# Up-projection of a Strassen-Winograd feed-forward: sums of products accumulated in PSUM onto copies placed by ScalarE, with product 1 of the next feature ahead of products 4 and 3

## The chip, the core and the metric

The kernel runs on one core of a Trainium2 chip. Its engines each work through a queue of their own in order and meet through semaphores: TensorE (matmuls, written PE in the profile; PEld are its weight loads), VectorE (DVE), ScalarE (ACT), GpSimd (POOL) and SyncE (SP), which here issues most of the DMA transfers. The metric is the device time of one execution in microseconds (us), lower is better; the time of a kernel is the median of several runs.

## The reference

One layer of a streaming encoder is computed for a prompt of 2048 tokens and for 8 x 16 sample tokens: RMSNorm and one combined projection, chunked attention and an mLSTM side by side, an output projection, and then a convolutional feed-forward network. The change concerns the first matmul of that network:

```python
def conv_ffn(h, buf, w_up, w_conv, b_conv, w_down):      # h: tokens x 1024, w_up: 1024 x 5632
    u = h @ w_up
    ext = concatenate([buf, u], axis=1)
    y = b_conv + sum(ext[:, j:j + S] * w_conv[j] for j in range(3))   # causal depthwise convolution
    gate, up = split(y, 2, axis=-1)
    return (gelu(gate) * up) @ w_down, ext[:, S:]
```

with RMSNorm before and after it and a residual sum. All values are float32.

## The kernel before, in words

Float32 accuracy is reached with three matmuls per product: each operand is split into a high part (float32r) and the remainder, and `mm3` adds high x high, high x low and low x high (lines 95, 96 and 97 of the profile).

*Stages.* The input projection, attention and mLSTM run first, then the output projection (`project`), and beside its end the feed-forward's operands are made. The feed-forward (from line 1263 on) runs over three token blocks, b = 0, 1, 2, of 6, 6 and 5 tiles of 128 tokens. In each block the up-projection loops over 22 features f of 128 columns of the gate and 128 of the up half; its result goes through convolution and GELU and is stored to DRAM (`gd`). Then the down-projection reads it back, in two halves.

*Seven products.* For each f the 1024 x 256 weights and the tokens are cut into 2 x 2 quarters, and four quarters of u come out of seven products (Strassen's scheme in Winograd's form) instead of eight. A product is 4 x 3 = 12 matmuls onto 384 columns (320 in block 2). The token side of the products (`B[P1]` to `B[P3]`) is made once a block; in block 0 the operands of P5, P2, P4 and P3 are kept in DRAM and split late (`late_B`, lines 1151 and 1152). The weight side needs three raw blocks (P1, P2, P4) and four sums of blocks, `ws`. In block 0 VectorE forms the sums (line 1282), and SP stores them (`wsd`) and the later blocks load them from there. The raw float32 blocks and sums sit in 11 `quad` buffers of SBUF and are split into high (ScalarE, line 1265) and low part (VectorE, line 1266) by `load_up`, two groups per feature: P1, P6, P7, P5, then P2, P4, P3. Three sets of buffers hold split groups.

*Sums of products.* With U2 = P1 + P6 the quarters are: gate first half P1 + P2; gate second half U2 + P5 + P3; up first half U2 + P7 + P4; up second half U2 + P7 + P5. Before, ScalarE copies P1 to SBUF (`x1`, line 1489), VectorE adds P6 (`x2`, line 1491) and P7 (`x3`, line 1493). P2 is accumulated in PSUM onto P1, P4 onto P7, P3 onto P5, and VectorE adds x2 or x3 to what stands there (lines 1419 and 1508) on the way to the SBUF tiles `uu` (up) and `ug` (gate); the first half of `ug` is a ScalarE copy (line 1506).

*Convolution.* `conv` copies the halo on GpSimd (lines 1430 and 1435), does one ScalarE activation (line 1438), two VectorE steps (1439 and 1440), and a GELU for the gate (1442). Line 1514 multiplies the two.

*Order.* The programme is written with Tile: it records the operations in the order of the code, and a planner with a timeline of its own decides the order in each engine's queue, so products of neighbouring features are interleaved on TensorE. PSUM has eight banks: two for `a` (tag mm), two for P6's sum (tag sm), two pairs for P7 and P5 (tag big). The down-projection uses mm and big again.

Of the kernel before, what the change touches and what calls it, by code (L numbers as in the profile page):

```python
# [10 lines left out]
F32 = mybir.dt.float32  # L11
# [6 lines left out]
P = 128  # L18
# [26 lines left out]
def hymba_step(ctx: ExitStack, tc: tile.TileContext, I: dict, O: dict):  # L45
# [1224 lines left out]
    def load_quads(b, f, g):  # L1270

        src = lambda i: I["w_up"][f][:, i * 512:(i + 1) * 512]
        if b == 0 and g == 0:
            q = []
            for i in range(4):
                q.append(quad(f"wu{f}_{i}"))
                nc.sync.dma_start(q[i], src(i))
            a11, a12, a22, a21 = q
            s1, s2, s3, s4 = [quad(f"ws{f}_{i}") for i in range(4)]
# [3 lines left out]
            for i, o in enumerate((s2, s3, s1, s4)):  # L1283
                nc.sync.dma_start(wsd[f][:, i * 512:(i + 1) * 512], o)
            raws[f] = [a12, a22, s4]
            return [a11, s2, s3, s1]
        if b == 0:
            return raws.pop(f)
        kept = lambda i: wsd[f][:, i * 512:(i + 1) * 512]
        out = []  # L1290
        for i, s_ in enumerate([[src(0), kept(0), kept(1), kept(2)], [src(1), src(2), kept(3)]][g]):
            r = quad(f"wu{b}_{f}_{g}_{i}")
            nc.sync.dma_start(r, s_)
            out.append(r)
        return out

    def load_up(b, f, g, quads=None):
        n = 2 * f + g
        nm = f"{b}_{f}_{g}"
# [7 lines left out]
        for (h, l), r in zip(at, quads or load_quads(b, f, g)):  # L1307
            split(h, l, r)
        return at
# [75 lines left out]
    pend = [load_up(0, 0, 0)]  # L1385
    late_B()
    pend.append(load_up(0, 0, 1))
# [15 lines left out]
    for b, tiles in enumerate(FBLOCKS):  # L1403
# [13 lines left out]
        def second(u, x, acc):  # L1417

            add = lambda o, c, v=lambda t: t: nc.vector.tensor_tensor(o, v(x[:, c]), v(acc[:, c]), op=ALU.add)  # L1419
            if not last:  # L1420
                add(u[:, 2 + n:2 + 2 * n], slice(0, n))
                return
            add(u[:, 2 + n + 64:2 + n + 192], slice(0, P))
            add(u[:, 2 + n:2 + n + 64], slice(2 * P, n))
            us = u[:, 2 + npr:2 + ln].rearrange("p (b s) -> p b s", b=DB)
            add(us[:, :, 2:DS + 2], slice(P, 2 * P), lambda t: t.rearrange("p (b s) -> p b s", b=DB))
# [18 lines left out]
        def ahead_of(i):  # L1445
            if i < 2 * NF:
                pend.append(load_up(b, i // 2, i % 2))
            elif i == 2 * NF:
                pend.append(load_down(0, 0))
# [27 lines left out]

        for f in range(NF):
            w = pend.pop(0)
            ahead_of(2 * f + 2)  # L1480
# [3 lines left out]
            nm = f"{b}_{f}"  # L1484
            a, d_, ec = ps_mm(f"ua{nm}"), ps_sm(f"ub{nm}"), ps_big(f"uec{nm}")
            e, c = ec[:, 0:512], ec[:, 512:1024]
            x1, x2, x3 = [p4.tile([P, 384], F32, tag="x", name=f"x{i}_{nm}", bufs=3) for i in range(3)]
            product(P1, w[0], a)
            nc.scalar.copy(x1[:, :n], a[:, :n])
            product(P6, w[1], d_)  # L1490
            nc.vector.tensor_tensor(x2[:, :n], x1[:, :n], d_[:, :n], op=ALU.add)
            product(P7, w[2], e)
            nc.vector.tensor_tensor(x3[:, :n], x2[:, :n], e[:, :n], op=ALU.add)
            product(P5, w[3], c)
            uu = u_tile(f"uu{nm}")
            second(uu, x3, c)
            w = pend.pop(0)
            ahead_of(2 * f + 3)
# [5 lines left out]
            ug = u_tile(f"ug{nm}")  # L1504
# [3 lines left out]
            nc.vector.tensor_tensor(uu[:, 2:2 + n], x2[:, :n], e[:, :n], op=ALU.add)  # L1508
# [16 lines left out]
        for dh in range(2):  # L1525
# [9 lines left out]
            for c in range(6):  # L1535
                wh, wl = pend
                if c < 5:
                    pend = load_down(dh, c + 1)
                elif dh == 0:
                    pend = load_down(1, 0)  # L1540
                elif not last:
                    quads = [load_quads(b + 1, 0, i) for i in range(2)]
                    pend = [load_up(b + 1, 0, 0, quads[0])]
# [53 lines left out]
        if not last:  # L1597
            while ahead.step():
                pass
            pend.append(load_up(b + 1, 0, 1, quads[1]))  # L1600
# [94 lines left out]
```

## Time and profile before

| what | value |
|---|---|
| median of 3 runs | 2796.26 us (2793.03 to 2800.73) |
| span of the profiled execution | 2784.7 us; its time beyond the span is not given on the page, and the median of the runs is 11.6 us longer |
| TensorE busy | 2723.8 us, 98% of the span |
| VectorE busy | 1876.3 us, 67% |
| ScalarE busy | 1409.1 us, 51% |
| mean granted clock of TensorE | 0.998 |
| up-projections of blocks 0, 1, 2 | about 1313 to 1641, 1836 to 2154 and 2342 to 2626 us |

The page gives busy time by engine, the granted TensorE clock in slices, DMA queues, the chain of work that ended last, and groups of instructions by source line (`out<-in`, count, busy us, mean ns of one, idle time before them and what ended it). The trace answers further questions: busy time in chosen stretches, who waited for whom, and the instructions in order of time. A busy TensorE counts pipelined matmuls, so its rate is read from the distance of two starts.

### The profile page before, as it was taken

The page shows a single profiled execution, that of the slowest core. Times are in us where ns is not written, and L with a number is a line of the kernel's source. Part 1 is how long each engine was busy: PE and PEld are TensorE (multiplying, and loading weights), DVE is VectorE, ACT ScalarE, POOL GpSimd, SP SyncE. Part 2 cuts the span into 40 slices and gives each one's busy share as a digit, 9 for nine tenths or more (in the row PEclk, how much of TensorE's full clock was granted, in tenths as well). Part 3 has the DMA queues.
Part 4 walks back from the last instruction along what each step waited for, and adds up shares of the span by engine and source line. Part 5 has one row for each costly group of instructions (what it writes and reads, how often), then busy time and mean ns, then how long its engine had stood idle before and what let it go on. Part 6 is the DMA issues. An engine that isn't in the chain of part 4 may idle for free.

```text
span 2784.7 us, 47088 instructions
## 1 busy us (share of the span) xinstructions
PE 2723.8 (98%) x16587; PEld 2548.3 (92%) x16587; DVE 1876.3 (67%) x3447; ACT 1409.1 (51%) x2836; POOL 437.4 (16%) x895
## 2 busy tenths in 40 slices
PE   8999999999999999999999999999999999999998
PEld 7899999998899998888999988899999878999887
DVE  5344455656556668666999986457877864888855
ACT  4355555644356666544454555345455543555543
POOL 1000010212000003244111110011111310222220
PEclk9999999999999999999999999999999999999999
DMA  5544355557555555356655455644544774555585
GB/s 185 155 119 136 103 174 162 164 157 217 162 173 148 144 179 171 107 176 227 187 172 167 167 176 174 219 142 153 160 152 141 276 263 152 172 179 180 192 309 190
DMA packets 311883, 486.05 MB, mean 175 GB/s; under 512 B 55426, under 2 KB 150622, under 8 KB 311518
## 3 DMA queue, kind: packets, MB, share of 16 engines
q1 hardware_dynamic: 271134, 442.92, 50.1%
q10 hardware_dynamic: 38592, 33.83, 3.6%
q0 software_dynamic: 1920, 6.29, 0.6%
q8 instruction: 130, 2.13, 0.3%
q14 instruction: 107, 0.88, 0.1%
HBM read 359.36 MB, written 126.70 MB: 175 GB/s over the span
## 4 chain that ended last, share of the span: by engine, by line
PE 55%; DVE 2%; DMA 1%; issue 1%; ACT 1%; POOL 1%; SPq 0%; DVEq 0%; POOLq 0%; ACTq 0%
PE uec L95 6%; PE uec L96 6%; PE uec L97 6%; PE dn L97 4%; PE dn L96 4%; PE dn L95 4%; PE ua L97 3%; PE ua L95 3%; PE ua L96 3%; PE dnm L97 2%; PE dnm L95 2%; PE dnm L96 2%; PE wo L97 2%; PE wo L95 2%; PE wo L96 2%; PE ub L96 1%
## 5 line engine op out<-in xcount | busy, mean ns | idle before, releaser
L95 PE MATMUL uec<-B,wuh 128*128 128x384 f32 (+1 forms) x720 | 234.9, 328 | 2.2 <-DVE uu L1419 1.1
L96 PE MATMUL uec<-B,wuh 128*128 128x384 f32 (+1 forms) x720 | 235.1, 327 | 0.0
L97 PE MATMUL uec<-B,wul 128*128 128x384 f32 (+1 forms) x720 | 233.9, 327 | 0.0
L1266 DVE TENSOR_TENSOR gl<-gr,gh 128x768 fp32r<-128x768 f32 (+3 forms) x141 | 120.4, 863 | 145.8 <-ACT gh L1265 144.5
L1265 ACT CAST gh<-gr 128x768 fp32r<-128x768 f32 (+3 forms) x141 | 102.0, 735 | 200.1 <-PE dn L96 183.2
L1265 ACT CAST wuh<-wu 128x512 fp32r<-128x512 f32 x255 | 141.7, 617 | 112.1 <-PE uec L96 103.2
L95 PE MATMUL dn<-wdh,gh 128*128 128x512 f32 x466 | 182.4, 391 | 2.3 <-DVE ug L1419 2.3
L96 PE MATMUL dn<-wdl,gh 128*128 128x512 f32 x466 | 183.4, 394 | 0.0
L97 PE MATMUL dn<-wdh,gl 128*128 128x512 f32 x466 | 167.9, 396 | 0.0
L1266 DVE TENSOR_TENSOR wul<-wu,wuh 128x512 fp32r<-128x512 f32 x255 | 164.6, 683 | 2.8 <-DMA x2d<-mx 2.8
L393 DVE CUSTOM_DVE_ANT_0 tmp<-s,nb 128x640 f32<-128x640 f32 (+4 forms) x128 | 94.4, 737 | 96.6 <-PE s L383 94.8
L95 PE MATMUL vo<-wi_h,hT 128*128 128x256 f32 x544 | 155.1, 285 | 0.6 <-DVE mt L199 0.6
L97 PE MATMUL vo<-wi_h,hT 128*128 128x256 f32 x544 | 155.6, 286 | 0.0
L96 PE MATMUL vo<-wi_l,hT 128*128 128x256 f32 x544 | 154.8, 285 | 0.0
L95 PEld LDWEIGHTS uec<-B,wuh 128*128 128x128 f32 x720 | 135.0, 188 | 4.2 <-DVE uu L1419 1.6
L95 PE MATMUL qk<-hT,wi_h 128*128 128x384 f32 (+1 forms) x384 | 128.7, 335 | 7.4 <-ACT qk_st L224 6.6
L96 PEld LDWEIGHTS uec<-B,wuh 128*128 128x128 f32 x720 | 135.2, 188 | 0.2
L97 PEld LDWEIGHTS uec<-B,wul 128*128 128x128 f32 x720 | 135.1, 188 | 0.0
L406 DVE TENSOR_TENSOR ptl<-pt,pth 128x640 fp32r<-128x640 f32 (+4 forms) x128 | 93.6, 737 | 57.1 <-ACT pth L405 56.0
L394 ACT ACTIVATE tmp<-tmp,mn 128x640 f32<-128x640 f32 (+4 forms) x128 | 97.6, 762 | 64.6 <-DVE mn L393 61.9
L96 PE MATMUL qb<-hT,wi_h 128*128 128x384 f32 (+1 forms) x384 | 127.8, 333 | 0.0
L96 PE MATMUL qk<-hT,wi_h 128*128 128x384 f32 (+1 forms) x384 | 127.6, 332 | 0.0
(412 smaller groups left out, 8873.0 us busy)
## 6 DMA issues: line engine op xcount, KB each, us to landing
wu<-in_w_up SPq DMA_DIRECT2D x220, 256.0 KB, 4.1
wu<-wsd SPq DMA_DIRECT2D x176, 256.0 KB, 4.2
wdr<-in_w_down SPq DMA_DIRECT2D x132, 256.0 KB, 5.6
gr<-gd SPq DMA_DIRECT2D x78, 384.0 KB, 3.6
wi_raw<-in_w_in SPq DMA_DIRECT2D x52, 512.0 KB, 4.0
wsd<-ws SPq DMA_DIRECT2D x88, 256.0 KB, 2.8
gd<-g SPq DMA_DIRECT2D x44, 384.0 KB, 3.5
kraw<-kTd SPq DMA_DIRECT2D x112, 128.0 KB, 3.2
```

The lines of the kernel that those rows point to most:

```text
L95: nc.tensor.matmul(out, ah, bh, start=start, stop=False, skip_group_check=onto)
L96: nc.tensor.matmul(out, ah, bl, start=False, stop=False, skip_group_check=onto)
L97: nc.tensor.matmul(out, al, bh, start=False, stop=stop, skip_group_check=onto)
L393: nc.vector.tensor_tensor_reduce(o_, s_, b_, 1.0, 3e38, ALU.add, ALU.min, accum_out=mn)
L394: nc.scalar.activation(tmp[:, :n], tmp[:, :n], AF.Exp, bias=mn, scale=-1.0, accum_out=rsum[:, i % 4, hh:hh + 1])
L406: nc.vector.tensor_tensor(s.ptl[:, sl, qc], ptv, s.pth[:, sl, qc], op=ALU.subtract)
L1265: nc.scalar.copy(h, r)
L1266: nc.vector.tensor_tensor(l, r, h, op=ALU.subtract)
```

## The change

1. The sums U2, U2 + P5 and so on are no longer added by VectorE. The copy of P1 goes from PSUM to PSUM, into the first bank of a `big` pair (`dc`), and P6 is accumulated onto it. ScalarE copies that sum (U2) into the second bank, and P5 is accumulated onto it. P4 is accumulated onto the first bank, P3 onto the second. P7 has a bank of its own (tag sm) and ScalarE copies it to SBUF (`p7`).
2. VectorE keeps two adds per feature: p7 + second bank (after P5) and p7 + first bank (after P4). The second half of `ug` is a ScalarE copy after P3.
3. Product 1 of feature f + 1 and its copy are written before P4 and P3 of feature f. So the weight groups are cut anew: P6, P7, P2, P5 of a feature, then P1 of the next with P4 and P3. In block 0 the block of P1 is loaded with its group, before the other raw blocks of its feature.
4. Before block 0 four matmuls write the four banks of the `big` tiles once with start=True (`mark`), so that later matmuls without it add to what stands there.
5. `quad` has 12 buffers instead of 11, `row` 6 instead of 4; the room comes from `dynamic_dma_scratch_size=4096`, a smaller area for the descriptors of GpSimd's DMAs.

```diff
 def quad(name):
-    return ffn.p3.tile([P, 512], F32, tag="q", name=name, bufs=11)
+    return ffn.p3.tile([P, 512], F32, tag="q", name=name, bufs=12)
 def row(name):
-    return ffn.p3.tile([P, D], F32, tag="yq", name=name, bufs=4)
+    return ffn.p3.tile([P, D], F32, tag="yq", name=name, bufs=6)
...
+    GROUPS_UP = [[(P1, 0), (P6, 0), (P7, 0), (P2, 0)], [(P5, 0), (P1, 1), (P4, 0), (P3, 0)]]
+    for f_ in range(1, NF):
+        GROUPS_UP.append([(P6, f_), (P7, f_), (P2, f_), (P5, f_)])
+        GROUPS_UP.append([(P1, f_ + 1)] * (f_ + 1 < NF) + [(P4, f_), (P3, f_)])
...
+    def first_quads(i, f):
...
+        if i == P1:
+            get(P1, 0)
+        elif i == P6:
+            a12, a22, a21 = get(P2, 1), get(P4, 2), get(None, 3)
+            a11 = raws["a11"] if f else raws[P1, 0]
+            s1, s2, s3, s4 = [quad(f"ws{f}_{x}") for x in range(4)]
...
-        def second(u, x, acc):
-            add = lambda o, c, v=lambda t: t: nc.vector.tensor_tensor(o, v(x[:, c]), v(acc[:, c]), op=ALU.add)
+        def halves(u, x, acc):
...
+        def first(f):
+            a, dc = ps_mm(f"ua{b}_{f}"), ps_big(f"udc{b}_{f}")
+            product(P1, W.pop((P1, f)), a)
+            nc.scalar.copy(dc[:, :n], a[:, :n])
+            return a, dc[:, 0:512], dc[:, 512:1024]
+
+        if b == 0:
+            for i in range(2):
+                t = ps_big(f"mark{i}")
+                for x in range(2):
+                    nc.tensor.matmul(t[:, x * 512:x * 512 + 384], B[P1][:, 0, 0, :P], B[P1][:, 0, 0, :],
+                                     start=True, stop=True)
...
-            product(P1, w[0], a)
-            nc.scalar.copy(x1[:, :n], a[:, :n])
-            product(P6, w[1], d_)
-            nc.vector.tensor_tensor(x2[:, :n], x1[:, :n], d_[:, :n], op=ALU.add)
-            product(P7, w[2], e)
-            nc.vector.tensor_tensor(x3[:, :n], x2[:, :n], e[:, :n], op=ALU.add)
-            product(P5, w[3], c)
-            second(uu, x3, c)
+            product(P6, W.pop((P6, f)), d_, onto=True)
+            nc.scalar.copy(c[:, :n], d_[:, :n])
+            product(P7, W.pop((P7, f)), e)
+            nc.scalar.copy(p7[:, :n], e[:, :n])
+            product(P2, W.pop((P2, f)), a, onto=True)
+            nc.scalar.copy(ug[:, 2:2 + n], a[:, :n])
+            product(P5, W.pop((P5, f)), c, onto=True)
+            for o, x, y in halves(uu, p7, c):
+                nc.vector.tensor_tensor(o, x, y, op=ALU.add)
...
-            product(P2, w[0], a, onto=True)
-            nc.scalar.copy(ug[:, 2:2 + n], a[:, :n])
-            product(P4, w[1], e, onto=True)
-            nc.vector.tensor_tensor(uu[:, 2:2 + n], x2[:, :n], e[:, :n], op=ALU.add)
-            product(P3, w[2], c, onto=True)
-            second(ug, x2, c)
+                nxt = first(f + 1)
+            product(P4, W.pop((P4, f)), d_, onto=True)
+            nc.vector.tensor_tensor(uu[:, 2:2 + n], p7[:, :n], d_[:, :n], op=ALU.add)
             yu = conv(uu, 1, f)
+            product(P3, W.pop((P3, f)), c, onto=True)
+            for o, _, y in halves(ug, None, c):
+                nc.scalar.copy(o, y)
             yg = conv(ug, 0, f)
...
-    nc = bacc.Bacc("TRN2", target_bir_lowering=False, num_devices=1)
+    nc = bacc.Bacc("TRN2", target_bir_lowering=False, num_devices=1, dynamic_dma_scratch_size=4096)
```

More of the change, by code (lines that the diff above doesn't have):

```diff
@@ L1541, in hymba_step @@
                 elif not last:
-                    quads = [load_quads(b + 1, 0, i) for i in range(2)]
-                    pend = [load_up(b + 1, 0, 0, quads[0])]
+                    quads = [load_quads(b + 1, i) for i in range(2)]
+                    pend = [load_up(b + 1, 0, quads[0])]
                 ks = list(range(4 * c, 4 * c + (4 if c < 5 else 2)))
```

97 lines of the change are left out of this document (53 added, 44 removed).

## The prediction

> **What bounds the kernel now.** I read the page first, then busy time by stage for the feed-forward part (it starts at 1313 us), then TensorE's waits there.
>
> ```profile
> span 2784.7 us, 47088 instructions
> ...
> PE 2723.8 (98%) x16587; PEld 2548.3 (92%) x16587; DVE 1876.3 (67%) x3447; ACT 1409.1 (51%) x2836; POOL 437.4 (16%) x895
> ```
>
> ```profile
> core 0: us, PE busy (x) PEld busy (x) DVE busy (x) ACT busy (x) POOL busy (x), PEclk, DMA share, GB/s
> 1313.00:1641.00 328.00, 322.00 (x1827) 318.55 (x1825) 302.79 (x457) 167.79 (x266) 61.74 (x87) 0.99 0.54 179
> 1641.00:1836.00 195.00, 193.23 (x865) 157.51 (x864) 110.03 (x152) 94.51 (x158) 6.71 (x22) 1.00 0.55 181
> 1836.00:2154.00 318.00, 318.00 (x1826) 317.91 (x1825) 246.19 (x366) 163.19 (x270) 42.99 (x96) 1.00 0.48 154
> 2154.00:2342.00 188.00, 186.85 (x837) 151.25 (x836) 120.16 (x156) 88.56 (x150) 36.99 (x46) 1.00 0.68 231
> 2342.00:2626.00 284.00, 283.56 (x1904) 280.91 (x1902) 244.50 (x493) 160.17 (x284) 64.43 (x182) 1.00 0.56 177
> 2626.00:2785.00 159.00, 148.00 (x636) 119.34 (x636) 89.40 (x129) 60.06 (x107) 30.61 (x41) 0.99 0.72 253
> ```
>
> Rows one, three and five are the up-projections of blocks 0, 1 and 2, the part that the change rewrites. TensorE is busy for 318.00 of 318 us in block 1 and 283.56 of 284 in block 2: nothing can be won there unless matmuls go away, and none does. Block 0 alone has a hole, 6 us, and there VectorE is busy for 302.79 of 328 us (92%), because it also forms the weight sums. Stage edges apart, the whole possible gain lies in block 0. Its waits:
>
> ```profile
> engine line waited for: us in total, times, longest us
> PE ua L97 <- DVE wul L1266: 3.0, 2, 1.6
> PE uec L95 <- DVE uu L1419: 1.1, 1, 1.1
> PE uec L95 <- DVE ug L1419: 1.0, 1, 1.0
> PE ub L97 <- DVE wu L1266: 0.6, 1, 0.6
> ...
> PE uec L95 <- DVE x L1493: 0.3, 1, 0.3
> PE uec L95 <- DVE uu L1508: 0.2, 1, 0.2
> ```
>
> These six rows are the up-projection's: 6.2 us, each wait ended by VectorE. The matmul pitch and the worst stall, from the timeline of TensorE, and that stall's clock, by windows:
>
> ```profile
> 1639.67 0.34 PE L96 MATMUL uec<-B,wuh 128*128 128x384 f32 x1
> ...
> 1640.88 0.34 PE L97 MATMUL uec<-B,wul 128*128 128x384 f32 x1
> ```
>
> ```profile
> 1387.08 0.42 PE L95 MATMUL uec<-B,wuh 128*128 128x384 f32 x1 [0.96 <-DVE ug L1419]
> ...
> 1389.06 0.69 PE L97 MATMUL ua<-B,wul 128*128 128x384 f32 x1 [1.39 <-DVE wul L1266]
> ```
>
> ```profile
> 1389.00:1392.20 3.20, 3.14 (x10) 3.14 (x11) 3.20 (x7) 0.38 (x1) 0.51 (x1) 0.54 0.68 210
> ```
>
> Seven starts apart is 1.21 us, so 0.173 us a matmul, 2.08 us a product of 12, 14.5 us a feature. After 0.96 and 1.39 us of waiting the granted clock was 0.54 for 3.2 us, which lost 3.2 x 0.46 = 1.5 us more. So block 0 loses 6.2 + 1.5 = 7.7 us. [...]
>
> What the worst stall and the next one followed, in the chain of waits:
>
> ```profile
> 1378.67 6.98 DMA wu<-in_w_up
> ...
> 1386.85 0.95 DVE g L1514
> ...
> 1388.41 0.61 DVE wul L1266
> 1389.06 0.69 PE ua L97
> ```
>
> ```profile
> 1514.25 5.42 DMA wu<-in_w_up
> ```
>
> A weight load took 6.98 us to land, VectorE stood before the weight sum that needs it, and then had its queue to work off.
>
> **The change, part by part.** Costs of what moves, block 0's rows by shape, VectorE then ScalarE:
>
> ```profile
> L1491 DVE TENSOR_TENSOR x<-x,ub 128x384 f32<-128x384 f32 x22 | 12.0, 547 | 0.1
> L1493 DVE TENSOR_TENSOR x<-x,uec 128x384 f32<-128x384 f32 x22 | 12.0, 545 | 0.0
> L1419 DVE TENSOR_TENSOR ug<-x,uec 128x384 f32<-128x384 f32 x21 | 11.5, 549 | 4.4 <-PE uec L97 4.3
> L1152 DVE TENSOR_TENSOR B<-B 128x1536 fp32r<-128x1536 f32 x4 | 6.8, 1745 | 0.0
> ```
>
> ```profile
> L1442 ACT ACTIVATE y<-y 128x768 f32<-128x768 f32 x20 | 16.9, 847 | 53.1 <-DVE y L1440 53.1
> ...
> L1489 ACT COPY x<-ua 128x384 f32<-128x384 f32 x22 | 10.5, 479 | 16.0 <-PE ua L97 16.0
> ```
>
> *Adds removed, copies added.* Per feature VectorE loses three adds, 1.64 us, 36 us over block 0's 22 features: 303 - 36 = 267 of 328 us, 81%. ScalarE gains three copies. A copy from PSUM to PSUM is not in the trace; the nearest row is L1489's of the same width, PSUM to SBUF, 0.479 us, and I take that (bounds: half of it, and the 0.847 us of a row twice as wide, L1442's): 22 x 3 x 0.48 = 32 us, 168 + 32 = 200 us, 61%, at the upper bound 68%. In block 2 the upper half of ug takes three small copies in place of three small adds. Neither engine becomes the bound by its sum. Worth on the path: only the VectorE waits after block 0's start, 0.96 + 1.39 + 1.1 + 0.3 + 0.2 = 3.9 us, and the clock's 1.5: 5.4 us. They began with late loads, so they are not sure to go; but a VectorE with 19% to spare works off its queue, and the rearranged groups (the twelfth quad buffer, product 1's block loaded one group ahead) let the third raw block be fetched about one group, 7 us, sooner. I take 4.3 of the 5.4; the ends are 0 and 5.4.
>
> *New waits: P1 -> copy -> P6, and P6 -> copy -> P5.* Two round trips in each of 66 features. TensorE's queue behind the waiting matmul is in order, so all later products wait with it. A trip costs the pipeline's tail (0.34 - 0.17), the start of the copy and the copy. The start is seen here:
>
> ```profile
> 1843.69 0.34 PE L97 MATMUL ua<-B,wul 128*128 128x384 f32 x1
> ...
> 1844.07 0.48 ACT L1489 COPY x<-ua 128x384 f32<-128x384 f32 x1 [1.18 <-PE ua L97]
> ```
>
> 0.04 us after the end, so with as much at the other end 0.17 + 0.04 + 0.48 + 0.04 = 0.73 us. In the built order 23 or more other matmuls stand between, mostly 24 (two products, 4.15 us) to 36, past the first features of each block. Cover left: 3.4 us. What can eat it is ScalarE's own order: a copy behind a GELU that waits for VectorE's convolution. Those waits (ScalarE, up-projections 0, 1, 2 in turn):
>
> ```profile
> ACT y L1442 <- DVE y L1440: 53.1, 17, 5.1
> ```
>
> ```profile
> ACT y L1442 <- DVE y L1440: 14.5, 13, 1.7
> ```
>
> ```profile
> ACT y L1442 <- DVE y L1440: 21.2, 13, 3.0
> ```
>
> Means 3.1, 1.1 and 1.6 us, longest 5.1, 1.7 and 3.0: only block 0 can pass 3.4. With less on VectorE the waits should shorten, and in the built order the GELU belongs to an older feature, whose convolution has mostly run. I take +0.7; the ends are 0 and 22 x (5.1 + 0.73 - 4.15) = 37 us.
>
> *Starts of blocks 1 and 2.* There only one product (2.08 us) stands between the first P1 and P6, so 1.35 us of cover, and ScalarE is still squaring the down-projection's rows, here before:
>
> ```profile
> 1841.40 0.64 ACT L1344 ACTIVATE junk<-fr 128x512 f32<-128x512 f32 x1
> ```
>
> One square ahead of the copy fits, three do not. I take +0.3 a block, +0.6; the ends are 0 and the whole product twice, 4.2.
>
> *Start of block 0.* Four mark matmuls, 4 x 0.173 = +0.7 us on TensorE. The four late operands are split on VectorE (L1152, 1.745 us each). The first was needed after five products, now after four, 2.1 us sooner; in the new order ScalarE and VectorE have less else in between. Before, the waits at this place were 1.6 + 0.6 = 2.2 us. Ends: -2.2 if they vanish, +2.1 if all of the lost cover shows. I take +0.6, nearer to the upper end than the middle is, because VectorE is the engine waited for.
>
> *The rest, at nothing.* SP issues the same transfers; product 1's block moves ahead of four sums and their stores. POOL copies halos as before, the gate's now first; it is busy for 62 of 328 us. Smaller descriptor scratch concerns POOL's 24 output stores in the down stages, where POOL is busy for 7 of 195 and 37 of 188 us; if one waited there, 150 us of idle cover it. More row buffers can only start loads earlier. At the end of each block the last down-projection sums wait for the evacuation of P3, now a ScalarE copy: 0.48 for 0.55 us, +/-1 us over three edges.
>
> **Sum:** -4.3 + 0.7 + 0.6 + 0.7 + 0.6 = -1.7 us on a span of 2784.7, so 2783.0. The page gives no more of that execution than its span; the median of the runs, 2796.26, is 11.6 us above it, and I keep that distance: 2794.6 us.
>
> **Rivals.**
> 1. *ScalarE's order stalls TensorE (slower).* Copies stand behind GELUs, and it decides as soon as GELU waits pass 3.4 us. For: 17 waits of 3.1 us on average in block 0. Against: VectorE gets 19% spare. If half of the 17 last 5.1 us, 8.5 x 1.7 = 14 us, in place of 0.7: 2794.6 + 13.3 = 2808 us. Chance 0.17.
> 2. *All waits go, edges included (faster).* Block 0's 7.7 and the later edges:
>
> ```profile
> PE dnm L95 <- ACT gh L1265: 1.8, 2, 1.5
> PE dn L95 <- DVE ug L1419: 1.6, 2, 1.4
> ```
>
> 3.4 us more, by the added quad and row buffers; with 0.7 for the marks -10.4: 2786 us. Against: the edges' work is unchanged. Chance 0.13.
> 3. *The stalls are the loads' and stay.* Both chains hold a late load that the lighter VectorE does not hasten. Without the 4.3: 2799 us. Chance 0.20.
> The forecast itself has 0.50.
>
> **How the numbers follow.** Within 0.3% (8.4 us, about what a measurement of this kernel can tell from no change; its three runs spread over 7.7 us) lie the forecast and rival 3: 0.70. Slower by more: rival 1, 0.17. Faster by more: rival 2, 0.13. The range runs from rival 2's 2786 less 1 us to 2805, most of the way to rival 1; the copies' upper end of 37 us is left outside.
>
> **What would show it.** Right: VectorE at some 267 us and ScalarE at 200 in block 0's up-projection, TensorE's waits there under 4 us, no row of a matmul of udc waiting for ScalarE by more than a us in total, and no window at half clock. Wrong: many waits of udc matmuls for the copies at L1504 or L1525, with GELU waits above 3 us ahead of them; a wait over 3 us at block 0's first P2 or P5; or blocks 1 and 2 no longer without a wait.

## The result, and the profile after

The changed kernel takes 2799.29 us (median of 20 runs, 2793.89 to 2807.54) against 2794.68 us for the kernel before, measured beside it (20 runs, 2792.06 to 2800.90): a ratio of 1.0015, 95% interval 1.0009 to 1.0022. It is slower by 4.6 us, where 1.7 us less was forecast. The time lies inside the forecast range, and the difference is smaller than the 0.3% that was called measurable; twenty runs of each resolve it all the same, and its sign is the wrong one.

Its profiled execution has a span of 2794.9 us. The spans of single executions mislead:

```profile
core 0: 2784.7 us, clock 0.998
```

```profile
core 0: 2796.1 us, clock 0.994
```

Both rows, from the view of spans and mean granted clock, are of the kernel *before*: the first is the execution that the prediction read, the second another one. The lost clock, 0.002 of 2785 us against 0.006 of 2796 us, makes 11 us, which is the difference of the spans. In the first execution TensorE reached its first up-projection matmul at 1313.45 us, in the second at 1323.72, with the same instructions up to there. So up to that matmul a single profile is worth 10 us of chance, and kernels are compared from that matmul on. The stages of five kernels, three of which come below (each figure is the distance between two starts in the timeline of TensorE: the first up-projection matmul of a block, the first of the down-projection after the block's last one, or the end):

| us | block 0 up | down | block 1 up | down | block 2 up | down | sum |
|---|---|---|---|---|---|---|---|
| before (mean of two traces) | 338.8 | 184.0 | 329.2 | 183.7 | 278.2 | 158.0 | 1471.9 |
| changed (mean of two traces) | 340.3 | 184.3 | 331.5 | 183.6 | 280.0 | 157.7 | 1477.3 |
| copies alone (e7) | 334.3 | 184.2 | 331.1 | 183.3 | 280.2 | 159.0 | 1472.1 |
| and VectorE at the block ends (e8) | 335.8 | 183.8 | 330.8 | 183.0 | 279.0 | 158.4 | 1470.7 |
| and the add moved (e15) | 331.9 | 183.8 | 330.3 | 184.6 | 279.0 | 156.7 | 1466.2 |

The changed kernel loses 5.4 us there, and 0.7 us for the marks ahead of it: 6.1 us by the traces, 4.6 us by the medians. Busy time by stage, in the changed kernel's first trace (the cut points are its own stage starts):

```profile
core 0: us, PE busy (x) PEld busy (x) DVE busy (x) ACT busy (x) POOL busy (x), PEclk, DMA share, GB/s
1318.00:1648.00 330.00, 324.06 (x1837) 321.45 (x1837) 275.91 (x395) 195.01 (x336) 61.41 (x88) 0.99 0.54 179
...
1842.00:2164.00 322.00, 321.15 (x1839) 320.11 (x1838) 220.40 (x306) 190.56 (x339) 44.02 (x97) 1.00 0.50 154
...
2357.00:2628.00 271.00, 270.22 (x1840) 269.38 (x1839) 206.98 (x369) 179.17 (x381) 68.21 (x182) 1.00 0.57 176
```

The work moved about as forecast: VectorE from 303 to 276 us in block 0 (267 was forecast), ScalarE from 168 to 195 (200). TensorE still stands for 6 of 330 us in block 0, but elsewhere than before. Its waits there, and then at the ends of blocks 0, 1 and 2:

```profile
PE ua L96 <- DVE B L1152: 2.8, 1, 2.8
PE ue L97 <- DVE wu L1266: 1.1, 1, 1.1
PE ua L95 <- ACT B L1151: 1.1, 1, 1.1
PE udc L95 <- DVE uu L1534: 0.7, 1, 0.7
```

```profile
PE dn L95 <- ACT ug L1549: 1.9, 1, 1.9
```

```profile
PE h2T_pt L1093 <- DVE x2r L1085: 1.2, 1, 1.2
PE udc L95 <- DVE uu L1534: 0.7, 1, 0.7
```

```profile
PE dn L95 <- ACT ug L1549: 2.0, 1, 2.0
PE udc L95 <- DVE uu L1534: 0.8, 1, 0.8
```

None of the 3.9 us of waits that block 0 had after its start is left. The first three rows are all of the start: 5.0 us, against 2.2 before. The clock behind them, by windows:

```profile
1331.40:1338.30 6.90, 4.85 (x14) 4.34 (x15) 6.26 (x5) 3.50 (x6) 1.90 (x2) 0.51 0.54 211
```

For 6.9 us TensorE had 0.51 of its clock; it was busy for 4.85 us of them, so some 2.4 us were lost (4.85 x 0.49). Windows of 3.4 us at half clock also stand behind the ends of blocks 0 and 2 in both of its traces; of before's two, one has such a window, behind block 2. In the changed kernel's first trace they start at 1659.05 and 2638.67 us. Place by place for block 0: -3.9 of waits and -1.5 of clock, then +2.8 at the start, +2.4 of clock behind it, and at the end +1.3 for the first down-projection sum (1.95 against 0.65) and about as much as before around it. That is +1.1; the two pairs of stage lengths say +1.5. The 0.65 us are in TensorE's timeline of the kernel before:

```profile
1652.39 0.50 PE L95 MATMUL dn<-wdh,gh 128*128 128x512 f32 x1 [0.65 <-DVE ug L1419]
```

Blocks 1 and 2 lose 2.2 and 1.8 us, most of it at their ends (0.7 us in block 1 lie at 2104 us, in four gaps that the trace gives no wait for).

What the worst wait hangs on, in the chain of waits, which gives start, us and what:

```profile
1324.75 1.42 ACT B L1151
1326.17 2.08 ACT wuh L1265 x4
1328.25 0.37 ACT p L1527
1328.62 1.38 ACT B L1151
1330.02 3.24 DVE B L1152
1333.31 0.69 PE ua L96
```

The late operands are copied by ScalarE and split by VectorE in the order product 5, 2, 4, 3. That order was left from the kernel before, where product 5 came first. The changed kernel needs product 2's first. So product 2 stands on ScalarE behind the copy of an operand that is not yet wanted and behind four weight casts (that operand's split on VectorE is over 0.6 us before product 2's begins). And its own split takes 3.24 us, where the prediction priced it at 1.745 us. The reason shows when VectorE's and GpSimd's timelines are laid side by side:

```profile
1327.66 1.75 DVE L1152 TENSOR_TENSOR B<-B 128x1536 fp32r<-128x1536 f32 x1
1330.02 6.57 DVE L1152 TENSOR_TENSOR B<-B 128x1536 fp32r<-128x1536 f32 x3 [0.61 <-ACT B L1151]
```

```profile
1327.83 3.81 POOL L1027 TENSOR_TENSOR mx<-mx 128x1024 f32<-128x1024 f32 x1 [1.40 <-DVE mx L1026]
```

GpSimd's residual add of the last row starts 0.17 us after the first split and takes 3.81 us, where the same add for the two rows before it took 2.4 us; it ends at 1331.64. The second split starts inside it and ends 1.6 us after it, at 1333.25. The other two take 1.75 us again. When the add started, 1.58 us of the first split were left, and the add took 1.41 us more than 2.4; when the second split started, 1.62 us of the add were left, and the split took 1.48 us more than 1.75. So the lengths come out as if each of the two instructions had stood still for nearly all that was left of the other.

### The profile page after: what moved, and what is told of

Its sections match the earlier page's. It is cut to its first block, busy times and chain, and to the rows that moved or that the text cites. A ratio compares the mean times of both kernels' runs of the same rounds, so it can differ in the third digit from the quotient of the medians.

```text
span 2794.9 us, 46904 instructions
## 1 busy us (share of the span) xinstructions
PE 2732.2 (98%) x16591; PEld 2556.6 (91%) x16591; DVE 1790.6 (64%) x3205; ACT 1482.9 (53%) x3078; POOL 441.2 (16%) x895
## 4 chain that ended last, share of the span: by engine, by line
PE 56%; DVE 1%; DMA 1%; ACT 1%; issue 1%; POOL 1%; SPq 0%; DVEq 0%; POOLq 0%; ACTq 0%
PE udc L95 6%; PE udc L96 6%; PE udc L97 6%; PE dn L97 4%; PE dn L96 4%; PE dn L95 4%; PE ua L96 3%; PE ua L97 3%; PE ua L95 3%; PE dnm L97 2%; PE dnm L95 2%; PE dnm L96 2%; PE ue L97 2%; PE ue L96 2%; PE ue L95 2%; PE wo L97 2%
## 5 line engine op out<-in xcount | busy, mean ns | idle before, releaser
L95 PE MATMUL udc<-B,wuh 128*128 128x384 f32 (+1 forms) x720 | 235.7, 328 | 2.2 <-DVE uu L1534 2.2
L96 PE MATMUL udc<-B,wuh 128*128 128x384 f32 (+1 forms) x720 | 235.6, 327 | 0.0
L97 PE MATMUL udc<-B,wul 128*128 128x384 f32 (+1 forms) x720 | 235.3, 327 | 0.1
L96 PE MATMUL dn<-wdl,gh 128*128 128x512 f32 x466 | 184.6, 396 | 0.0
L95 PEld LDWEIGHTS udc<-B,wuh 128*128 128x128 f32 x720 | 135.5, 188 | 3.4 <-DVE uu L1534 3.3
L97 PEld LDWEIGHTS udc<-B,wul 128*128 128x128 f32 x720 | 135.4, 188 | 0.7 <-DVE wul L1266 0.7
L96 PEld LDWEIGHTS udc<-B,wuh 128*128 128x128 f32 x720 | 135.5, 188 | 0.1
L97 PE MATMUL qk<-hT,wi_l 128*128 128x384 f32 (+1 forms) x384 | 128.2, 334 | 0.0
```

Source lines behind the costliest of these rows:

```text
L95: nc.tensor.matmul(out, ah, bh, start=start, stop=False, skip_group_check=onto)
L96: nc.tensor.matmul(out, ah, bl, start=False, stop=False, skip_group_check=onto)
L97: nc.tensor.matmul(out, al, bh, start=False, stop=stop, skip_group_check=onto)
```

## The experiments

All ratios are against the kernel before, run on the same chip. The theory at the outset (A): the loss is three places, the start of block 0, the ends of the blocks, and the half clock behind both. Its rivals: ScalarE's copies cost it all along (B), or chance does. Further ones came up on the way and are named in the expectations.

**e0: the changed kernel again.**

> The changed kernel once more, beside the kernel before and the next three on one chip. Every theory expects the ratio of its first measurement, 1.0015 (1.0009 to 1.0022), some 4 us above the kernel before. What the profile should repeat, if the theory holds that the edit itself makes three kinds of loss (A): some 5 us of TensorE waits for VectorE at the start of block 0's up-projection, two waits of about 2 us for the ScalarE copy of ug at the ends of two blocks, and windows of 3.4 us at half clock behind both. By the rival (B) that these are chance of one execution, they should be shorter or absent in a second profile.

2797.33 us, ratio 1.0025 (1.0017 to 1.0034). The second trace repeats the first: waits of 1.13, 1.08 and 2.82 us at the start with 6.8 us of half clock behind them, 1.95 and 2.05 us at the ends of blocks 0 and 2, each stage within 0.8 us. The losses belong to the kernel and not to one execution.

**e1: six products ahead of the late operands.**

```diff
-    GROUPS_UP = [[(P1, 0), (P6, 0), (P7, 0), (P2, 0)], [(P5, 0), (P1, 1), (P4, 0), (P3, 0)]]
+    GROUPS_UP = [[(P1, 0), (P6, 0), (P7, 0), (P1, 1)], [(P2, 0), (P5, 0), (P4, 0), (P3, 0)]]
...
+            if f == 0:
+                take(1)
             product(P2, W.pop((P2, f)), a, onto=True)
```

> The changed kernel with the first two weight groups of block 0 regrouped, so that six products instead of four stand before the first product that needs a late operand; nothing else is changed. Theory A (the start lost its cover): the TensorE waits at the start of block 0, 5.0 us in the changed kernel's trace, fall to 2 us or less, the two half-clock windows behind them (3.4 us lost) go, and the median falls by 4 to 7 us, to a ratio of 0.999 to 1.000 against the kernel before. Rival B (the loss comes from ScalarE's added copies and the round trips all along the three blocks): the ratio stays at 1.0015.

2799.45 us, ratio 1.0032 (1.0020 to 1.0045): no gain over e0. The start did improve, and the half-clock windows there went, but block 0 took 339.8 us:

```profile
PE udc L95 <- DVE uu L1545: 2.3, 2, 1.9
PE dn L95 <- ACT ug L1549: 1.9, 1, 1.9
PE ue L97 <- DVE wul L1266: 1.5, 2, 0.8
PE udc L95 <- DVE uu L1534: 1.0, 2, 0.7
PE ua L96 <- DVE B L1152: 1.0, 1, 1.0
PE ua L95 <- ACT B L1151: 0.8, 1, 0.8
```

The last two rows are the start, 1.8 us in place of 5.0. What VectorE did not owe at the start it owes one feature later, for uu (1.9 us at 1349) and for weight splits at 1439 and 1616. "The start lost its cover" was right about the wait and wrong about the time.

**e2, e3: VectorE copies ug at the ends of the blocks; e3 with the start of e1.**

```diff
-                nc.scalar.copy(o, y)
+                (nc.vector.tensor_copy if f == NF - 1 else nc.scalar.copy)(o, y)
```

> The changed kernel, but the last feature of each block has the second half of ug copied by VectorE instead of ScalarE. Theory A: at the ends of the blocks ScalarE stands at three or four casts of down-projection weights of 1.66 us each when P3's sums are ready, VectorE does not; the two waits of 1.95 and 2.04 us shrink to 0.7 to 1.4 us each, the half-clock windows behind them become fewer, and the median falls by 1 to 5 us. Rival B: the waits at these places end with the weights, so that a wait of the same 2 us for ScalarE's casts takes their place and the time stays.

> Both edits together: regrouped start and VectorE's copy at the ends of the blocks. Theory A: the gains add up, 5 to 12 us below the changed kernel, so 1 to 8 us below the kernel before: a ratio of 0.997 to 0.9997, since what is left of the edit is the 4.3 us that VectorE's waits in block 0 cost, less 0.7 us for the marks. Rival B: no better than the changed kernel, 1.0015.

Ratios 1.0014 (1.0005 to 1.0022) and 1.0012 (1.0003 to 1.0020), where e0 has 1.0025 on that chip: 1.3 and 1.0 us less by the medians, but the intervals overlap. From the first up-projection matmul on, e2's trace is 1475.0 us long, against 1476.7 and 1477.9 in the changed kernel's two. In e2's trace the wait at the end of block 0 is

```profile
PE dnm L95 <- ACT gh L1265: 0.8, 1, 0.8
PE dn L95 <- DVE ug L1549: 0.7, 1, 0.7
```

and no half-clock window follows it. What the copy had waited for in the changed kernel is in ScalarE's timeline:

```profile
1655.99 1.66 ACT L1265 CAST wdh<-wdr 128x512 fp32r<-128x512 f32 x3 [4.12 <-PE udc L96]
1657.55 0.47 ACT L1549 COPY ug<-udc 128x384 f32<-128x384 f32 x1
```

Three weight casts, 1.66 us, stood ahead of a copy of 0.47 us in ScalarE's queue. By the traces the exchange takes back 1.8 to 2.9 of the 5.4 us lost; the medians alone don't settle it. e3 (forecast 0.997 to 0.9997) missed, as e1 did.

**e4, e7, e8: accumulation onto copies, the rest undone.** e4 restores the old weight groups and puts product 1 back at the head of its own feature; e7 also restores the three sizes; e8 adds the exchange of e2 to e7.

```diff
-            if f == 0:
-                nxt = first(0)
+            nxt = first(f)
...
-            else:
-                nxt = first(f + 1)
```

> The changed kernel with the weight groups of the kernel before and without running product 1 ahead: product 1 stands again at the head of its own feature, products 4 and 3 come before it; the accumulation onto ScalarE's copies stays. Only one product then stands between product 1 and product 6 in program order, though the built order has 23 to 25 other matmuls between most of them. If the round trips cost nothing wherever a product or two stand between (theory A), the steady parts of the blocks show no wait for the copies, the start of block 0 waits 2 us instead of 5, and the ratio falls to 0.999 to 1.001. If running ahead is what hides the trips (rival E), TensorE waits at product 6 or product 5 for ScalarE in many features, tens of us in all, and the ratio is above 1.003.

> The accumulation onto ScalarE's copies alone, with everything else of the edit undone: old weight groups, product 1 at the head of its own feature, 11 quad buffers, 4 row buffers, the default descriptor scratch. Theory C' (the sizes cost some 4 us in block 0 through another order of the same work, and the copies themselves gain): block 0's up-projection with its edge takes 335 to 338 us against 338.8 of the kernel before, and the ratio is 0.998 to 1.000. Rival F (the copies cost it, whatever the sizes: ScalarE's evacuation at the three block ends and the wait for uu's sum there): blocks 1 and 2 keep their 2 us each, block 0 gains nothing, and the ratio is 1.0015 or more.

> The same, with VectorE in place of ScalarE for the copy of the second half of ug in the last feature of each block. Theory C': about 1.5 us below the kernel with ScalarE's copy, as the same exchange gave on the changed kernel; a ratio of 0.997 to 1.000 against the kernel before, the waits of the first down-projection sums 0.65 to 0.8 us instead of 2. Rival F: 1.001 or more.

Ratios 1.0006 (0.9997 to 1.0015), 1.0014 (1.0004 to 1.0023) and 0.9997 (0.9987 to 1.0008). In none of them does TensorE wait for the copies of L1504 or L1525 (the numbers in these kernels differ by a few lines); running product 1 ahead is not what hides the trips, since the built order puts 22 or more other matmuls between most of them in either case. So rival E is out, and since e8 has all the copies and shows no loss, so is rival B. Theory A gave e4 a start with 2 us of waits; its trace has 4.4 us there (0.2, 1.7, 0.5 and 1.9), and block 0 takes 340.3 us. e7's waits from its first up-projection matmul to the end of block 0's edge:

```profile
PE ue L97 <- DVE wu L1266: 2.7, 1, 2.7
PE dn L95 <- ACT ug L1543: 1.9, 1, 1.9
PE udc L95 <- DVE uu L1529: 0.5, 1, 0.5
PE ua L95 <- ACT B L1151: 0.3, 1, 0.3
```

Nothing is left between the start and the end: in this trace block 0 is 4.5 us shorter than before, and blocks 1 and 2 are each 2 us longer. In e8, whose TensorE order is the same up to the end of block 0, the gain there is 3.0 us: a half-clock window follows its wait of 2.7 us, and none follows e7's. e8 takes back 0.3 and 1.2 us in blocks 1 and 2 and can't be told from the kernel before. Rival F is right about the ends, and wrong that block 0 gains nothing. By the medians e7 is 3.5 us behind the kernel before, as F forecast and theory C' did not; its one trace shows 0.9 us (0.2 in the stages, 0.7 for the marks).

**e5, e6, e9, e10: the sizes.** e6 is the kernel before with all three new sizes, e9 with the quads alone, e10 with the rows alone (both with the smaller scratch, which was not run alone; e10 has it and loses nothing); e5 is the changed kernel with the old ones.

```diff
-        return ffn.p3.tile([P, 512], F32, tag="q", name=name, bufs=11)
+        return ffn.p3.tile([P, 512], F32, tag="q", name=name, bufs=12)
```

> The kernel before with nothing changed but the three sizes: 12 quad buffers, 6 row buffers, descriptor scratch of 4096. In the five traces of the changed kernel and its variants TensorE reaches the up-projection 3.6 to 7.7 us later than in the one trace of the kernel before, though the instructions up to there are the same; most of it comes between 440 and 1040 us. Theory C (the sizes delay the earlier stages): this kernel also reaches the up-projection some 4 us late, and its ratio to the kernel before is 1.001 to 1.002. Theory D (the one trace of before was an undisturbed execution, the lateness there is chance that any execution has): ratio 1.0000, give or take 0.0008, though its single profile may be late as well.

> The changed kernel with the three sizes of the kernel before: 11 quad buffers, 4 row buffers, the default descriptor scratch. Theory C (the sizes delay the earlier stages): the median falls by some 4 us against the changed kernel, to a ratio of 1.000 to 1.001 against the kernel before, unless loads in block 0 become later in exchange. Theory D (the sizes do nothing there): the ratio stays at 1.0015 to 1.0025, or rises where the twelfth quad buffer was needed: then the profile shows more TensorE waits for weight sums in block 0.

> The kernel before with 12 quad buffers instead of 11 (and the smaller descriptor scratch that makes the room), 4 row buffers as before. With both sizes the ratio was 1.0015 and block 0's up-projection took 3.7 us longer. If the twelfth quad buffer is the cause, it is 1.001 to 1.002 again, with a wait of some 3 us for a weight sum's low part at the start of block 0 as there; if the row buffers are, it is 1.0000, give or take 0.0008.

> The kernel before with 6 row buffers instead of 4 (and the smaller descriptor scratch), 11 quad buffers as before. The counterpart of the kernel with the quad buffer alone: 1.001 to 1.002 if the row buffers are the cause, 1.0000 if the quad buffer is. In both, the earlier stages are free to be 0 to 10 us late in a single profile, which then says nothing about the sizes.

e6 1.0015 (1.0005 to 1.0025), e9 1.0029 (1.0019 to 1.0038), e10 0.9996 (0.9987 to 1.0005), e5 1.0049 (1.0030 to 1.0068). The twelfth quad buffer alone costs the kernel before as much as the whole edit, and not in the earlier stages, as Theory C had it; Theory D's 1.0000 for e6 is out too. By the traces block 0 takes 3.7 us more in e6 and 1.9 us more in e9; the rest of e9's 5.5 us lies in the down-projection of block 1 (2.1 us) and in block 2 (1.4 us), and its cause stays open. The two longest of e9's waits in block 0:

```profile
PE ua L97 <- DVE wul L1266: 3.7, 2, 3.0
PE uec L95 <- DVE x L1493: 2.1, 2, 1.4
```

The buffer changes no instruction. It changes the order in which the planner sets them. At the place where TensorE waited 1.6 us for a weight split before, it now waits 3.0 us: that split stands behind the late operands' splits, one of which takes 3.50 us here beside GpSimd's add of 3.85 us, and starts 19.4 us after the first up-projection matmul instead of 17.4 (in before's second trace). Taken away from the changed kernel together with the other two sizes, it costs far more (e5: block 0's up-projection 350.6 us, 10 us of half clock at its start). Between e4 and e7, which differ in the sizes alone, the medians show no gain, though e7's trace is 4 us shorter. So the buffer is neither good nor bad: each order meets the start of block 0 in its own way.

**b0: the kernel before again.**

> The kernel before once more, for a second profile. Theory D: the profile is 2788 to 2793 us long, with some of the lateness between 440 and 1040 us and more than two half-clock windows ahead of the tail. Theory C: it again reaches the up-projection at about 1313.5 us.

Ratio 1.0006 (0.9997 to 1.0016): no difference, as it must be, and a measure of what such a comparison tells apart. On the lateness its trace settles Theory D against C: 1323.72 us to the first up-projection matmul, 10.3 us later than in the first trace, and 6 half-clock windows up to there instead of 1, which is 8.5 us of it. (With 2796.1 us its span is even longer than D's 2788 to 2793.)

**e12, e13: product 2's operand first; e13 with VectorE at the ends.**

```diff
-        for i in (P5, P2, P4, P3):
+        for i in (P2, P5, P4, P3):
```

> The changed kernel with the late operands loaded and split in the order in which its products now need them: product 2's first, product 5's second (the code kept 5, 2, 4, 3 from the time when product 5 came first). Theory I (the loss at the start of block 0 is this order): the waits at the start fall from 5.0 us to some 2 us, with one half-clock window fewer or two, block 0's up-projection falls from 340 to 335 to 337 us, and the ratio from 1.0015-1.0025 to 1.0000-1.0010. Rival J (the twelfth quad buffer's order of work costs it, whatever operand comes first): the ratio stays at 1.0015 or above.

> Product 2's operand first, and VectorE's copy of the second half of ug at the ends of the blocks. Theory I with the gain of the exchange seen twice (about 1.3 and 3.9 us): a ratio of 0.998 to 1.000 against the kernel before, with block 0's up-projection at 334 to 336 us. Rival J: 1.0012, as with the regrouped start.

1.0012 (1.0003 to 1.0022) and 1.0006 (0.9997 to 1.0016). The wait for product 2's operand fell from 3.9 us in two pieces to 0.3, and no half-clock window is left at the start. But the built order changed with it, so that e12's block 0 still took 340.4 us, with new waits of 0.5 and 0.2 us for the round-trip copies, 0.7 us for product 5's split (3.27 us long beside the add) and 2.0 us for weight splits. Theory I holds for the wait, and rival J for the time of block 0; the ratio lies between their forecasts.

**e11: one instruction moved, all else equal.**

```diff
-            nc.gpsimd.tensor_tensor(xr, m, xr, op=ALU.add)
+            (nc.gpsimd if nxt else nc.vector).tensor_tensor(xr, m, xr, op=ALU.add)
```

> The changed kernel with one instruction moved: the last row's add of 128x1024 into the residual goes from GpSimd to VectorE; every other order on every engine stays. In the changed kernel that add runs from 1327.83 for 3.81 us, and the split of product 2's operand on VectorE takes 3.23 us beside it instead of 1.75. Theory G (the two engines block each other there, and TensorE's wait of 2.83 us at product 2 contains that 1.5 us): the split takes 1.75 us, TensorE's wait at product 2 falls by about 1 us although VectorE has 1.3 us more to do, and the kernel is 1 to 3 us faster if a half-clock window goes with it. Rival H (the long split is a matter of its data's place, or of the load): it takes 3.2 us again and the wait grows by 1.3 us.

2793.14 us, ratio 1.0010 (1.0001 to 1.0019). VectorE's timeline:

```profile
1327.66 1.75 DVE L1152 TENSOR_TENSOR B<-B 128x1536 fp32r<-128x1536 f32 x1
1329.33 1.22 DVE L1027 TENSOR_TENSOR mx<-mx 128x1024 f32<-128x1024 f32 x1
1330.46 5.09 DVE L1152 TENSOR_TENSOR B<-B 128x1536 fp32r<-128x1536 f32 x3
```

Three splits take 5.09 us in place of 6.57. TensorE's waits in block 0:

```profile
PE ua L96 <- DVE B L1152: 1.8, 1, 1.8
PE udc L97 <- DVE wul L1266: 1.4, 1, 1.4
PE ue L97 <- DVE wu L1266: 1.1, 1, 1.1
PE ua L95 <- ACT B L1151: 1.1, 1, 1.1
PE udc L95 <- DVE uu L1534: 0.7, 1, 0.7
PE ua L97 <- DVE wul L1266: 0.4, 1, 0.4
```

The wait at product 2 is 1.8 us in place of 2.8: Theory G to a tenth of a us. The next one, for a weight split, took up more than was won: the start waits 5.8 us in all, against 5.0. But the longest single wait is a us shorter, and no half-clock window stands at the start any more, nor behind block 0's end, where the 1.95 us wait is unchanged. By the traces the kernel is 4 to 5 us shorter from the first up-projection matmul on (1472.7 against 1476.7 and 1477.9). The ratio's interval overlaps with those of the changed kernel, so the medians alone do not settle the gain; the split's duration does settle the collision.

**e14, e15, e16: the repaired versions.** e14 is e8 with six row buffers; e15 is e8 with e11's move; e16 is e13 with it.

> The accumulation onto copies with the old groups, 11 quad buffers and VectorE's copy at the ends (0.9997 so far), with 6 row buffers, which alone came out at 0.9996. If the two are independent: 0.9985 to 1.000. If the six row buffers only looked harmless with the adds in place: above 1.000.

> The accumulation onto copies with old groups and old sizes and VectorE's copy at the block ends (0.9997 so far), with the last row's 128x1024 add on VectorE instead of GpSimd. There the add ran beside two weight splits, which took 3.49 us instead of 1.28, and TensorE waited 2.69 us for a later one. Theory G: the two splits take 1.3 us, the wait falls by some 0.9 us (2.2 saved less 1.3 for the add), and the ratio is 0.998 to 0.9995. Rival: what is gained there is given back at the next wait, and it stays at 0.9997.

> Product 2's operand first, VectorE's copy at the block ends (1.0006 so far), and the last row's add on VectorE. The split beside the add took 3.28 us instead of 1.75, and three waits near it lasted 0.3, 0.5 and 0.7 us. Theory G: at most 1 us less, a ratio of 0.9995 to 1.0005; by the rival that block 0's later waits and the 0.9 us at each block end are the rest of the loss, it stays above 1.000 and blocks 1 and 2 keep their 1.4 and 0.5 us.

e14 1.0001 (0.9991 to 1.0011), e16 0.9999 (0.9988 to 1.0009): neither can be told from the kernel before. e16 is the changed kernel with all three repairs. Within these intervals they take back its whole loss, which fits the start and the ends as its cause; the move of the add may also gain something of its own, as in e15. e15 beats both kernels: 2785.80 us against 2792.00, ratio 0.9974 (0.9964 to 0.9983). In e8 two weight splits beside the add took 3.49 us; in e15 the same two take 1.28. First e8's row, then e15's:

```profile
1324.34 3.49 DVE L1266 TENSOR_TENSOR wu<-ws,wu 128x512 fp32r<-128x512 f32 x2
```

```profile
1323.34 1.28 DVE L1266 TENSOR_TENSOR wu<-ws,wu 128x512 fp32r<-128x512 f32 x2
1324.55 1.22 DVE L1027 TENSOR_TENSOR mx<-mx 128x1024 f32<-128x1024 f32 x1
```

and its waits in block 0 and at its end are

```profile
PE udc L95 <- DVE uu L1529: 1.1, 2, 0.6
PE dn L95 <- DVE ug L1543: 0.7, 1, 0.7
PE ua L95 <- ACT B L1151: 0.5, 1, 0.5
PE udc L95 <- DVE uu L1539: 0.3, 1, 0.3
```

The 2.7 us wait of e7 and e8 is gone whole, not by the 0.9 us worked out ahead, and a few TensorE rows changed places as well, which may be why; block 0 is 6.9 us shorter than in the kernel before. The add was not moved in the kernel before alone, though the same collision stands there: beside the add one of its 128x512 splits takes 2.44 us, where it takes 0.68 alone. So the rival that the move by itself gives all of e15's gain is not tested, and how much of the gain needs the copies stays open: e8, which has them without the move, shows no gain over the kernel before.

## Why the prediction was wrong

*VectorE's waits in block 0, -4.3 (ends 0 and -5.4).* Right, and at its better end. All of 3.9 us and the half-clock window behind them are gone in both traces of the changed kernel; e7, where the copies and the marks are all that is new, has a block 0 shorter by 4.5 us, its slower end included (e8's and e14's, with the same 2.7 us wait and a half-clock window behind it, by 3.0). But the lighter VectorE alone doesn't ensure it: in e1, with the same copies in another order, 4.2 us of such waits stand past the start. Rival 3, that these waits belong to the loads, is out: the loads of weights took longer to land after the change (5.1 us in the median against 4.1 over the whole kernel, 5.1 against 4.9 in block 0's up-projection), and the waits went all the same.

*Round trips, +0.7.* The copies from PSUM to PSUM took 0.47 us, where 0.48 was taken. The waits were zero in the changed kernel, where no row names L1504 or L1525 as what TensorE waited for; 0.7 to 3.2 us in e12 and e5, whose orders put less between. The cover of 3.4 us was enough, and GELU's waits for VectorE fell from 53.1 to 22.2 us in block 0, the longest from 5.1 to 2.4, so rival 1 did not come about. (ScalarE's wait ahead of a convolution, for uu, grew from 13.8 to 27.8 us there, the longest 4.3, and stalled TensorE as little.) *Starts of blocks 1 and 2, +0.6:* no wait there.

*Marks, +0.7.* As worked out.

*Start of block 0, +0.6 (ends -2.2 and +2.1).* **This is the step that failed first.** It counted products ahead of "the first late operand", four instead of five, and did not ask which operand that is and where it stands in the order of splits. It is product 2's, second in that order. And it took 1.745 us a split from a row that is a mean over four executions without a neighbour on GpSimd. The waits were 5.0 us, +2.8, beyond the upper end, and the half clock behind them, which the sum priced for the old stalls and not for new ones, made some 2.4 us more. One of the prediction's own signs of being wrong, a wait over 3 us at block 0's first product 2, came with it, in two pieces of 1.06 and 2.83 us.

*"The rest, at nothing".* **The second.** The copy at the ends of the blocks was priced by its own duration, 0.48 for 0.55 us, and not by ScalarE's queue, where 1.66 us of casts stand ahead of it: 1.3 us for block 0, 0 to 0.6 for block 2 (2.04 us against 1.43 and 2.04 in before's two traces). With the wait for uu (0.7 to 0.8 us three times; in two of the places 0.5 us for weights stood before) and for x2r in block 1 (1.2 us), the ends are most of the 4 us that blocks 1 and 2 lose. "More row buffers can only start loads earlier" was true of the rows, 0.9996. For the quads a gain of loads was counted into the first term; that a planner sets another order once a buffer more is free was not considered, and it is worth 0.15% (with the rows) and 0.29% (alone) in the kernel before. What it costs or saves inside the changed kernel no run isolates.

*The 11.6 us between the span and the median* were carried over as if they lay around the profiled execution. A time is 1.7 us above its own span; the rest was that this execution had less half clock (a granted clock of 0.998, where before's second trace has 0.994). It shifts both kernels alike, so it cost the forecast time little and the difference nothing, but it was not what it was taken for.

*The clock's 1.5 us* came from a window at half clock behind two waits, 2.35 us together, in the kernel before. The changed kernel's windows have waits just ahead of them too: in its first trace those from 1331.37, 1659.05 and 2638.67 us have waits of 1.06 and 2.83 us (the first window starts inside the second wait), of 1.95 and of 2.04 us. But a wait is no sure sign: the 1.95 us at the end of block 0 are followed by a window in the changed kernel and not in e11, and the 2.7 us at the start by one in e8 and not in e7. What went with the windows is counted at the end of the last section.

Sum by what was measured, from the traces: marks +0.7, block 0 +1.5, its down-projection +0.3, blocks 1 and 2 +2.2 and +1.8, the other down-projections -0.4: +6.1 us, of which the medians show 4.6.

## What to carry to other kernels

Where a planner or a buffer count sets the order, an edit's cost at the one tight place (here the first products of block 0) can't be read off the edit: look up in the built order which operand is wanted first and what stands ahead of its producers on their queues, and expect each repair to move the next wait. Price a moved instruction by the queue it joins and not by its own duration (here 1.66 us of casts ahead of a copy of 0.47 us), and a VectorE instruction by what GpSimd does beside it (here 3.23 us for a split inside GpSimd's add and 1.75 us without it). Compare stages, not spans: 10 us of chance in the stages ahead hid both the loss and its cause here.

## What the runs showed of the hardware

Where a VectorE split with both operands in SBUF and GpSimd's 128x1024 add ran side by side, each held the other up. The 128x1536 split took 1.75 us alone, and where it started inside the add 3.23 us in the changed kernel, 3.28 in e13 and 3.50 in e9. The add took 2.40 us alone (the kernel before, from 1306.37 us) and 3.81 us in the changed kernel, where it started just behind a split; with the add on VectorE (e11) it took 1.22 us there and the splits 1.75. A VectorE add with one operand in PSUM ran inside GpSimd's add in its usual 0.55 us: L1491, 128x384, in the kernel before, at 1320.26 us, inside the add that runs from 1319.82 us for 2.79 us, and L1493 in e6 and e9. The late split ended 1.6 us after the add did in the changed kernel, nearly its own length; in the kernel before the 128x512 split inside the add (2.44 us, 0.68 alone) ended 0.55 us after it. Both are as after a full stop.

Ahead of the kernel's end half-clock windows all last 3.41 us, or a multiple of it (6.83 us from 1331.37 us on in the changed kernel), and in each of the 20 traces all of them start on one grid of 3.413 us: in the first trace of the kernel before at 108.51, 1388.51 and, at the end, 2781.14 us, in the changed kernel's at seven places from 82.09 to 2792.27 us, all within 0.001 us of the grid. With each trace cut into the cells of its grid, from 60 us on, the sum of TensorE's idle time in a cell goes with what comes next. A half-clock window followed all 84 full-clock cells with 1.88 us or more of it, 20 of 119 with 1.30 to 1.88 us, and none of 15706 with less. In those two traces alone, their ends included, it followed all 9, 1 of 10 and none of 1569. That fits the cases above. e8's wait of 2.7 us fell into one cell, in which TensorE was busy for 0.72 of 3.41 us; e7's was cut by the grid into two, with 1.88 and 2.01 us busy. The cell at the end of block 0 has 1.46 us busy in the changed kernel, and in e11 the wait is cut into cells with 2.72 and 2.16 us busy. The grid lies elsewhere in each execution (counted from the span's start, 2.69 us past a multiple of 3.413 us in the first trace of the kernel before and 0.17 us in the changed kernel's). So by these counts the price of a stall of 2 to 3 us is its length, or its length and up to 1.7 us more (half of a 3.41 us window), by chance. In the stages before the up-projection the number of windows differed from 1 to 6 between two executions of the same kernel; the five more are 8.5 of the 10.3 us that set the two apart there.
